# Dividing attention probabilities in the transposing product instead of on GpSimd

## Chip, cores, metric

One core of a Trainium2 chip. The time is that of one execution on the device in microseconds. Engines are named as the profile names them: PE is TensorE's matmul, PEld its weight load, DVE is VectorE, ACT ScalarE, POOL GpSimd, SP SyncE.

## What is computed

A trunk of two layers over 1024 tokens of width 1024. Layer 0 mixes tokens with softmax attention (8 query heads of 128, 2 key/value heads), layer 1 with a gated delta rule; a gated MLP follows each. The change lies in the attention of layer 0:

```
q = apply_axial_rope(rmsnorm(q, q_norm), rope) * (ATT_HEAD_DIM ** -0.5)
k = apply_axial_rope(rmsnorm(k, k_norm), rope)
...
s = jnp.einsum('bqkgd,bskd->bkgqs', q_blk, k)
p = jax.nn.softmax(s, axis=-1)
return jnp.einsum('bkgqs,bskd->bqkgd', p, v)
...
o = o * jax.nn.sigmoid(gate.astype(jnp.float32))
```

## The kernel before

The program runs its stages one after the other on one core; a scheduling layer sets each engine's order of instructions from the order in which they are recorded, the dependences and priorities. Large products are made of pairs: a float32 value is split into a high part of type float32r and a low part (`split`, lines 108 to 110: a cast on ScalarE, a subtraction on VectorE), and three products high x high, high x low, low x high are added in PSUM. Products of plain float32 tiles are also used, for instance at line 513 in the delta-rule layer, where weights and moving operand are 128x128 tiles.

The attention's core is the class `Heads`. A group is one head and one half of its 1024 queries, so there are 16; a group has four tiles of 128 queries. For each tile `scores` (from line 1231) makes the 128x1024 scores by six products of 512 columns (line 1243), VectorE takes their maximum (1246) and a tiny product of it (1247), ScalarE the exponential with its row sums (1249), VectorE the reciprocal of the sums (1251), and GpSimd multiplies the 128x1024 tile p by it (1252). `run` (from 1271) goes over the groups and, in each, over 8 blocks of 128 keys. In blocks 0, 1, 3 and 4 it makes one tile of scores of the next group; in each block it transposes the four 128x128 pieces of p into one PSUM bank (1285), and the bank is split into the pair ph, pl (1288, recorded at lines 109 and 110). `weigh` (1254 to 1269) multiplies a pair with the values by three products of 512 columns (1263), two blocks after the pair was made (`LAG = 2`). After the eighth block VectorE multiplies by the gate (1268), and the result is split.

The first group's scores are made before `run`, between the gate projections of heads 1 to 4 (line 320); the gates are emptied from PSUM by ScalarE at line 291. Tiles of the names base4 to base7 (the profile prints "base") hold the first group's p.

```
for i in range(4):
    nc.tensor.transpose(out=pt[:, i * P:(i + 1) * P], in_=self.ps[g][i][:, j * P:(j + 1) * P],
                        identity=t.ident)
```

Of the kernel before, what the change touches and what calls it, by code (L numbers as in the profile page):

```python
# [9 lines left out]
F32 = mybir.dt.float32  # L10
F32R = mybir.dt.float32r
F16 = mybir.dt.float16
AF = mybir.ActivationFunctionType
ALU = mybir.AluOpType
# [4 lines left out]
P = 128  # L19
# [22 lines left out]
class Trunk:  # L42
    def __init__(self, ctx, tc, ap):
        self.tc, self.nc, self.ap = tc, tc.nc, ap
        nc = self.nc
        pool = lambda **k: ctx.enter_context(tc.tile_pool(reuse_waits="tile", **k))
        tc.cur_priority += 1000000
        self.const = pool(name="const", bufs=1)
        self.dram = pool(name="dram", bufs=1, space=DRAM)
        self.mm = pool(name="mm", bufs=2, space=PSUM)  # L50
        self.ring = "sp"
        self.wp = pool(name="wp", bufs=3)
        self.bp = pool(name="base", bufs=1)
        self.ones = self.const.tile([P, 1], F32, name="ones")
        nc.vector.memset(self.ones, 1.0)
        self.ident = self.load("ident", [P, P])
        self.power = self.const.tile([P, 16], F32, name="power")
        nc.vector.memset(self.power, -0.5)
        self.gain_mix = self.load("norm_mix", [P, 2, KT])
        self.gain_ffn = self.load("norm_ffn", [P, 2, KT])  # L60
        self.gain_final = self.load("norm_final", [P, KT])
# [785 lines left out]
    def run(self, out, start, stop):  # L847
        nc, tc = self.nc, self.tc
        self.psum = self.banks(sp=4)
        if start > 0:  # L850
            if start % 2:
                self.open_operands()
            self.open_h()
            for k in range(KT):
                nc.sync.dma_start(out=self.h[k], in_=self.ap["xT"][k])
                for i, hs in enumerate(HALVES):
                    self.squares(self.h[k][:, hs], hs, k)
        stages = [self.attention, lambda: self.ffn_layer(0), self.gdn, lambda: self.ffn_layer(1)]
        for f in stages[start:stop]:
            f()  # L860
        if stop == 5:
            self.norm(self.h, self.gain_final,
                      out=lambda k, i, y: nc.sync.dma_start(out=out[k][:, HALVES[i]], in_=y))
        else:
            for k in range(KT):
                nc.sync.dma_start(out=out[k], in_=self.h[k])
        self.hp.close()
        if stop % 2 and stop < 5:
            self.ops.close()
        self.psum.close()  # L870
# [335 lines left out]
class Heads:  # L1206


    def __init__(self, trunk, qd, gd, ks, vh, vl, scale, tmp):
        self.t, self.nc = trunk, trunk.nc  # L1210
        self.qd, self.gd, self.ks, self.vh, self.vl, self.scale, self.tmp = qd, gd, ks, vh, vl, scale, tmp
        self.groups = [(h, i) for h in range(NH) for i in range(2)]
        self.qs, self.sgs, self.ps, self.accs, self.waiting, self.ys = {}, {}, {0: []}, {}, [], []

    def queries(self, g, pair):
        h, half = self.groups[g]
        q = self.tmp.tile([P, S], F32, name="t")[:, :H2]
        self.nc.sync.dma_start(out=q, in_=self.qd[h][:, HALVES[half]])
        self.qs[g] = pair
        self.t.split(q, *pair)  # L1220
# [10 lines left out]
    def scores(self, g, p):  # L1231

        nc = self.nc
        h, half = self.groups[g]
        i = len(self.ps[g])
        self.ps[g].append(p)
        kh, kl = self.ks[h // 4]
        qh, ql = self.qs[g]
        acc = self.t.big()
        tok = slice(i * P, (i + 1) * P)  # L1240
        for n, (a, b) in enumerate(((qh, kh), (qh, kl), (ql, kh))):
            for s in HALVES:
                nc.tensor.matmul(acc[:, s], lhsT=a[:, tok], rhs=b[:, s], start=n == 0, stop=n == 2)
        i += 4 * half
        m = self.tmp.tile([P, 4], F32, name="m", bufs=14)
        nc.vector.tensor_reduce(out=m[:, 0:1], in_=acc, op=ALU.max, axis=AX.X)
        nc.vector.scalar_tensor_tensor(out=m[:, 1:2], in0=m[:, 0:1], scalar=-1.0, in1=self.scale[:, h, i:i + 1],
                                       op0=ALU.mult, op1=ALU.mult)
        nc.scalar.activation(out=p, in_=acc, func=AF.Exp, scale=self.scale[:, h, i:i + 1], bias=m[:, 1:2],
                             accum_out=m[:, 2:3])  # L1250
        nc.vector.reciprocal(out=m[:, 3:4], in_=m[:, 2:3])
        nc.gpsimd.tensor_scalar(out=p, in0=p, scalar1=m[:, 3:4], scalar2=1.0, op0=ALU.mult, op1=ALU.mult)

    def weigh(self):

# [15 lines left out]
    def run(self, olo, qp, ptp):  # L1271
        nc, t = self.nc, self.t
        self.ys = [(t.base(h), olo.tile([P, S], F32R, name=f"ol{h}")) for h in range(NH)]
        self.gate(0)
        for g, (h, half) in enumerate(self.groups):
            if g + 1 < len(self.groups):
                self.queries(g + 1, t.pair(qp, "q", H2))
                self.gate(g + 1)
            self.ps[g + 1] = []
            for j in range(NC):  # L1280
                if g + 1 < len(self.groups) and j in (0, 1, 3, 4):
                    self.scores(g + 1, qp.tile([P, S], F32, name="p", bufs=8))
                pt = t.bank()
                for i in range(4):
                    nc.tensor.transpose(out=pt[:, i * P:(i + 1) * P], in_=self.ps[g][i][:, j * P:(j + 1) * P],
                                        identity=t.ident)
                self.waiting.append((g, j, t.pair(ptp, "p", H2)))
                t.split(pt, *self.waiting[-1][2])
                if len(self.waiting) > LAG:
                    self.weigh()  # L1290
            del self.ps[g]
        while self.waiting:
            self.weigh()
        return self.ys
# [97 lines left out]
```

## Time and profile before

| | us |
|---|---|
| median of 3 runs | 3449.74 (3447.62 to 3450.36) |
| the profiled execution | 3439.26 |
| its span in the profile | 3437.5 |
| attention's groups (in the profile) | 291 to 529 |

The span is what the instructions of the program take from the first start to the last end. In the rows, out<-in are the tiles written and read, xN the number of instructions merged or grouped, and <- in brackets what ended an engine's idle time. PE rows overlap, since products are pipelined; the distance from one start to the next is what one takes from the stream.

### The profile page before, as it was taken

What the parts mean: (1) busy time and instruction counts of PE and PEld (TensorE: products, weight loads), DVE (VectorE), ACT (ScalarE), POOL (GpSimd) and SP (SyncE); (2) the same over time, 40 slices, a digit from 0 to 9 for tenths busy, and PEclk for the clock granted to TensorE, in tenths of its full rate; (3) what the DMA queues carried; (4) which work ended last, traced back from release to release, by engine and by line L of the source; (5) the groups of instructions that cost most, each with busy time, mean ns of one, the idle gap of its engine ahead of it and who ended that gap; (6) DMA issues with size and microseconds to landing.
All of it is one profiled execution on the core that took longest, in us unless ns stands there. A gap on an engine that the chain in (4) does not pass through costs nothing. (4 is left out here: it accounts for less than half of the span.)

```text
span 3437.5 us, 54135 instructions
## 1 busy us (share of the span) xinstructions
PE 3247.3 (94%) x19690; PEld 2620.0 (76%) x19690; DVE 2495.2 (73%) x4235; ACT 1741.5 (51%) x3224; POOL 842.4 (25%) x919
## 2 busy tenths in 40 slices
PE   7999999899999998899999999999898989999998
PEld 6877788677777876677777777777676867777786
DVE  5335886887776875778778787877853787777695
ACT  4235664544454454565555556666532544544453
POOL 1111330444442002121221212222120144444100
PEclk9999999999999999999999999999999999999999
DMA  3331006333324642332342424334356623332743
GB/s 127 104 113 59 32 31 191 122 106 111 112 94 168 218 129 65 102 111 88 113 126 81 136 92 130 102 113 132 102 175 206 204 98 110 101 105 92 244 132 109
DMA packets 249802, 411.20 MB, mean 120 GB/s; under 512 B 25536, under 2 KB 76096, under 8 KB 249536
## 3 DMA queue, kind: packets, MB, share of 16 engines
q1 hardware_dynamic: 249536, 407.76, 36.6%
q8 instruction: 155, 2.54, 0.3%
q14 instruction: 111, 0.91, 0.1%
HBM read 294.80 MB, written 107.61 MB: 117 GB/s over the span
## 5 line engine op out<-in xcount | busy, mean ns | idle before, releaser
L134 PE MATMUL mm<-base,wh 128*128 128x512 f32 x1248 | 480.1, 412 | 10.0 <-ACT base L109 5.9
L109 ACT CAST wh<-w_raw 128x512 fp32r<-128x512 f32 x275 | 169.9, 619 | 296.7 <-PE mm L134 175.6
L110 DVE TENSOR_TENSOR wl<-w_raw,wh 128x512 fp32r<-128x512 f32 x275 | 193.2, 707 | 138.2 <-ACT wh L109 137.1
L134 PE MATMUL mm<-yh,wh 128*128 128x512 f32 x736 | 282.6, 413 | 5.3 <-ACT t L291 2.7
L134 PE MATMUL mm<-yh,wl 128*128 128x512 f32 x736 | 280.6, 410 | 1.0 <-DVE wl L110 1.0
L134 PE MATMUL mm<-yl,wh 128*128 128x512 f32 x736 | 279.3, 408 | 0.3 <-POOL yl L110 0.2
L134 PEld LDWEIGHTS mm<-base,wh 128*128 128x128 f32 x1248 | 238.3, 191 | 49.6 <-ACT base L109 6.3
L153 POOL TENSOR_TENSOR rs<-rs,power 128x8 f32<-128x8 f32 (+2 forms) x38 | 63.8, 1679 | 824.8 <-DVE rs L152 824.7
L134 PE MATMUL mm<-base,wl 128*128 128x512 f32 x624 | 257.3, 412 | 6.4 <-DVE wl L110 6.4
L703 POOL TENSOR_SCALAR kd<-c,yds 128x128 f32<-128x128 f32 x224 | 95.2, 437 | 635.0 <-PE cp L732 444.8
L109 ACT CAST wh<-a 128x512 fp32r<-128x512 f32 x164 | 101.8, 622 | 256.7 <-PE mm L134 122.6
L109 ACT CAST wh<-s 128x512 fp32r<-128x512 f32 x212 | 131.4, 620 | 183.6 <-PE sp L134 87.3
L134 PE MATMUL sp<-base,wh 128*128 128x512 f32 (+1 forms) x672 | 211.5, 372 | 12.6 <-ACT wh L109 12.6
L448 DVE SCALAR_TENSOR_TENSOR t<-mm,gdn_cw,t 128x1023 f32<-128x1023 f32 (+1 forms) x128 | 163.1, 1276 | 6.8 <-ACT t L445 6.1
L134 PEld LDWEIGHTS mm<-yh,wh 128*128 128x128 f32 x736 | 140.6, 193 | 29.3 <-ACT t L291 3.6
L134 PEld LDWEIGHTS mm<-yl,wh 128*128 128x128 f32 x736 | 140.8, 192 | 27.8 <-POOL yl L110 1.6
L134 PEld LDWEIGHTS mm<-yh,wl 128*128 128x128 f32 x736 | 140.8, 191 | 26.5 <-DVE wl L110 1.7
L134 PE MATMUL sp<-base,wl 128*128 128x512 f32 (+1 forms) x432 | 157.7, 365 | 1.4 <-DVE wl L110 0.9
L134 PEld LDWEIGHTS sp<-base,wh 128*128 128x128 f32 x672 | 127.7, 190 | 34.3 <-ACT wh L109 13.0
L110 DVE TENSOR_TENSOR wl<-s,wh 128x512 fp32r<-128x512 f32 x170 | 142.0, 836 | 12.3 <-ACT wh L109 12.2
L978 POOL TENSOR_TENSOR s<-a,a 128x512 f32<-128x512 f32 x80 | 108.5, 1356 | 159.0 <-DVE s L978 106.0
L134 PEld LDWEIGHTS mm<-base,wl 128*128 128x128 f32 x624 | 119.1, 191 | 27.2 <-DVE wl L110 7.2
(522 smaller groups left out, 9362.4 us busy)
## 6 DMA issues: line engine op xcount, KB each, us to landing
a<-in_ffn_up_dram SPq DMA_DIRECT2D x160, 256.0 KB, 2.8
c<-pk SPq DMA_DIRECT2D x128, 320.0 KB, 3.1
w_raw<-in_gdn_in_dram SPq DMA_DIRECT2D x100, 256.0 KB, 2.8
g_t<-t SPq DMA_DIRECT2D x88, 256.0 KB, 2.0
raw<-g_t SPq DMA_DIRECT2D x88, 256.0 KB, 2.6
w_raw<-in_gdn_out_dram SPq DMA_DIRECT2D x68, 256.0 KB, 3.6
g<-t SPq DMA_DIRECT2D x66, 256.0 KB, 2.1
raw<-g SPq DMA_DIRECT2D x66, 256.0 KB, 2.8
```

The source lines that it names most:

```text
L109: self.nc.scalar.copy(out=hi, in_=src)
L110: (engine or self.nc.vector).tensor_tensor(out=lo, in0=src, in1=hi.bitcast(F32), op=ALU.subtract)
L134: self.nc.tensor.matmul(acc if one else acc[:, hs], lhsT=a, rhs=y[:, hs], start=(first and not onto and k + t == 0), stop=(last and k == n ...
L153: nc.gpsimd.tensor_tensor(out=r, in0=v, in1=self.power[:, :w], op=ALU.pow)
L448: nc.vector.scalar_tensor_tensor(out=o, in0=a, scalar=c[:, i:i + 1], in1=o, op0=ALU.mult, op1=ALU.add)
L703: nc.gpsimd.tensor_scalar(out=kd[:, e], in0=kn, scalar1=col(self.yds, e), scalar2=1.0, op0=ALU.mult, op1=ALU.mult)
L978: e.tensor_tensor(out=s[i], in0=x, in1=z, op=op)
```

## The change

The division by the row sums leaves GpSimd. For each tile ScalarE scales the rows of the 128x128 identity by the reciprocals, which gives a diagonal matrix `inv` (eight buffers, two groups). The four pieces of p are no longer transposed against the identity but multiplied with that diagonal by an ordinary float32 product: p transposed times the diagonal is the transposed tile with each query's column divided by its sum.

```diff
--- before.py
+++ after.py
@@ -1211,6 +1211,7 @@
         self.qd, self.gd, self.ks, self.vh, self.vl, self.scale, self.tmp = qd, gd, ks, vh, vl, scale, tmp
         self.groups = [(h, i) for h in range(NH) for i in range(2)]
         self.qs, self.sgs, self.ps, self.accs, self.waiting, self.ys = {}, {}, {0: []}, {}, [], []
+        self.invs = {}
 
     def queries(self, g, pair):
         h, half = self.groups[g]
@@ -1249,7 +1250,9 @@
         nc.scalar.activation(out=p, in_=acc, func=AF.Exp, scale=self.scale[:, h, i:i + 1], bias=m[:, 1:2],
                              accum_out=m[:, 2:3])
         nc.vector.reciprocal(out=m[:, 3:4], in_=m[:, 2:3])
-        nc.gpsimd.tensor_scalar(out=p, in0=p, scalar1=m[:, 3:4], scalar2=1.0, op0=ALU.mult, op1=ALU.mult)
+        inv = self.tmp.tile([P, P], F32, name="inv", bufs=8)
+        nc.scalar.activation(out=inv, in_=self.t.ident, func=AF.Identity, scale=m[:, 3:4])
+        self.invs.setdefault(g, []).append(inv)
 
     def weigh(self):
 
@@ -1282,13 +1285,14 @@
                     self.scores(g + 1, qp.tile([P, S], F32, name="p", bufs=8))
                 pt = t.bank()
                 for i in range(4):
-                    nc.tensor.transpose(out=pt[:, i * P:(i + 1) * P], in_=self.ps[g][i][:, j * P:(j + 1) * P],
-                                        identity=t.ident)
+
+                    nc.tensor.matmul(pt[:, i * P:(i + 1) * P], lhsT=self.ps[g][i][:, j * P:(j + 1) * P],
+                                     rhs=self.invs[g][i], start=True, stop=True)
                 self.waiting.append((g, j, t.pair(ptp, "p", H2)))
                 t.split(pt, *self.waiting[-1][2])
                 if len(self.waiting) > LAG:
                     self.weigh()
-            del self.ps[g]
+            del self.ps[g], self.invs[g]
         while self.waiting:
             self.weigh()
         return self.ys
```

Two places where the order of instructions differs follow; the numbers in the names are buffers. The first is ScalarE in the middle of the attention stage, over half a group: first before, then of the change (p is an exponential, ph the high part of a transposed bank, qh that of the next queries, base2 or base3 that of a finished head).

```order
L1249 ACTIVATE p_3048,m_3056<-mm_3049,m_3056,scale_102 128x1024
L109 CAST ph_3093<-sp_3088 128x512
L109 CAST ph_3109<-sp_3104 128x512
L1249 ACTIVATE p_3074,m_3082<-mm_3075,m_3082,scale_102 128x1024
L109 CAST base2_2046<-t_3100 128x512
L109 CAST qh_3205<-t_3207 128x512
L109 CAST ph_3136<-sp_3131 128x512
L1249 ACTIVATE p_3117,m_3125<-mm_3118,m_3125,scale_102 128x1024
L109 CAST ph_3162<-sp_3157 128x512
L109 CAST ph_3174<-sp_3169 128x512
L1249 ACTIVATE p_3143,m_3151<-mm_3144,m_3151,scale_102 128x1024
```

```order
L1250 ACTIVATE p_3414,m_3422<-mm_3415,m_3422,scale_102 128x1024
L1254 ACTIVATE inv_3427<-ident_71,m_3422 128x128
L109 CAST ph_3461<-sp_3456 128x512
L1250 ACTIVATE p_3441,m_3449<-mm_3442,m_3449,scale_102 128x1024
L109 CAST ph_3477<-sp_3472 128x512
L1254 ACTIVATE inv_3454<-ident_71,m_3449 128x128
L109 CAST base3_2052<-t_3468 128x512
L109 CAST qh_3575<-t_3577 128x512
L109 CAST ph_3505<-sp_3500 128x512
L1250 ACTIVATE p_3485,m_3493<-mm_3486,m_3493,scale_102 128x1024
L109 CAST ph_3532<-sp_3527 128x512
L1254 ACTIVATE inv_3498<-ident_71,m_3493 128x128
```

An `inv` follows each exponential: one right behind its own, the others behind one cast of a bank.

The second place is VectorE in the same stage, around the low half of the queries (ql), first before, then of the change (the reduction is of the scores' maxima, pl the low part of a transposed bank).

```order
L1246 TENSOR_REDUCE m_2656<-mm_2649 128x1
L1251 RECIPROCAL m_2630<-m_2630 128x1
L110 TENSOR_TENSOR pl_2668<-sp_2662,ph_2667 128x512
L1247 SCALAR_TENSOR_TENSOR m_2656<-m_2656,scale_102 128x1
L110 TENSOR_TENSOR ql_2711<-t_2712,qh_2710 128x512
L110 TENSOR_TENSOR pl_2680<-sp_2674,ph_2679 128x512
L1251 RECIPROCAL m_2656<-m_2656 128x1
```

```order
L1247 TENSOR_REDUCE m_2648<-mm_2641 128x1
L110 TENSOR_TENSOR ql_2731<-t_2732,qh_2730 128x512
L1248 SCALAR_TENSOR_TENSOR m_2648<-m_2648,scale_102 128x1
L110 TENSOR_TENSOR pl_2661<-sp_2655,ph_2660 128x512
L1247 TENSOR_REDUCE m_2675<-mm_2668 128x1
L1252 RECIPROCAL m_2648<-m_2648 128x1
L1248 SCALAR_TENSOR_TENSOR m_2675<-m_2675,scale_102 128x1
L110 TENSOR_TENSOR pl_2688<-sp_2682,ph_2687 128x512
L1252 RECIPROCAL m_2675<-m_2675 128x1
```

ql stood behind the second tiny product and ahead of one bank's low part; now it stands ahead of the first tiny product, one bank earlier.

## Rows read from the trace of the kernel before

**Rows 1.** By stretches: start:end, length, busy us per engine (instructions), clock, DMA.

```profile
291.00:529.00 238.00, 232.85 (x1245) 188.93 (x1246) 204.50 (x353) 160.21 (x280) 68.24 (x60) 1.00 0.10 35
529.00:560.00 31.00, 30.07 (x133) 24.55 (x132) 15.97 (x24) 11.06 (x18) 0.00 (x0) 1.00 0.70 223
```

**Rows 2.** Waits in 291 to 529 us: us, times, longest.

```profile
ACT p L1249 <- DVE m L1247: 44.4, 56, 1.4
...
PEld sp L1263 <- DVE pl L110: 8.8, 17, 0.7
```

**Rows 3.** Groups in 291 to 529 us: count, busy us, mean ns, idle before.

```profile
L1252 POOL TENSOR_SCALAR p<-p,m 128x1024 f32<-128x1024 f32 x60 | 68.2, 1138 | 189.6 <-DVE m L1251 127.0 <-PE sp L1285 57.0 <-DVE m L1247 5.6
...
L1251 DVE RECIPROCAL m<-m 128x1 f32<-128x1 f32 x60 | 9.5, 158 | 9.7 <-ACT p L1249 9.7
```

**Rows 4.** Timeline of PE, four transposes: start us, length us, instructions merged.

```profile
513.69 0.60 PE L1285 MATMUL sp<-ident,p 128*128 128x128 f32 x4
514.04 0.48 PE L1263 MATMUL sp<-ph,vh 128*128 128x512 f32 x1
514.36 0.40 PE L1263 MATMUL sp<-pl,vh 128*128 128x512 f32 x1
514.60 0.39 PE L1263 MATMUL sp<-ph,vl 128*128 128x512 f32 x1
```

**Rows 5.** Timeline of PE at line 513, ordinary products of this shape.

```profile
1393.11 1.05 PE L513 MATMUL sp<-t 128*128 128x128 f32 x8
1393.92 0.48 PE L134 MATMUL mm<-base,wl 128*128 128x512 f32 x1
1394.23 0.39 PE L134 MATMUL mm<-yh,wl 128*128 128x512 f32 x1
...
1394.95 1.16 PE L513 MATMUL sp<-t 128*128 128x128 f32 x8
1395.86 0.48 PE L134 MATMUL mm<-base,wh 128*128 128x512 f32 x1
```

**Rows 6.** By source line: 513 (ordinary products), 1285 (transposes); min/median/max ns.

```profile
L513 PE MATMUL sp<-t x256: 270/275/426, 1386.6 to 2401.3; 128*128 128x128 f32 x128
...
L1285 PE MATMUL sp<-ident,p x480: 270/272/330, 304.3 to 526.7; 128*128 128x128 f32 x160
```

**Rows 7.** Timeline of PE: late products, first and last of twelve; last group.

```profile
334.55 0.50 PE L1263 MATMUL sp<-pl,vh 128*128 128x512 f32 x1 [0.20 <-DVE pl L110]
...
501.11 0.47 PE L1263 MATMUL sp<-ph,vh 128*128 128x512 f32 x1
501.86 0.50 PE L1263 MATMUL sp<-pl,vh 128*128 128x512 f32 x1 [0.28 <-DVE pl L110]
...
517.10 0.49 PE L1285 MATMUL sp<-ident,p 128*128 128x128 f32 x3
518.72 0.33 PE L1285 MATMUL sp<-ident,p 128*128 128x128 f32 x1 [1.13 <-POOL p L1252]
```

**Rows 8.** Timelines of VectorE and GpSimd, line 1247 with and without GpSimd.

```profile
347.90 0.59 DVE L1247 SCALAR_TENSOR_TENSOR m<-m,scale 128x1 f32<-128x1 f32 x1
...
347.36 1.13 POOL L1252 TENSOR_SCALAR p<-p,m 128x1024 f32<-128x1024 f32 x1 [2.58 <-DVE m L1251]
...
353.72 0.15 DVE L1247 SCALAR_TENSOR_TENSOR m<-m,scale 128x1 f32<-128x1 f32 x1
```

**Rows 9.** Timeline of PE behind the early transposes, two of four places.

```profile
227.46 0.49 PE L1285 MATMUL sp<-ident,base 128*128 128x128 f32 x3
228.85 0.73 PE L134 MATMUL mm<-yh,wh 128*128 128x512 f32 x2 [0.90 <-ACT t L291]
...
291.07 0.49 PE L1263 MATMUL sp<-ph,vh 128*128 128x512 f32 x1 [1.26 <-ACT ph L109]
```

**Rows 10.** Groups of ScalarE of the shape 128x128: count, busy us, mean ns.

```profile
L718 ACT ACTIVATE o<-cp,egc 128x128 f32<-128x128 f32 x112 | 35.5, 365 | 27.4 <-DVE r L714 16.4 <-PE mm L134 9.0 <-PE ip L674 1.2
...
L484 ACT ACTIVATE sq<-h 128x128 f32<-128x128 f32 x64 | 20.1, 313 | 1.2
```

## Prediction

> **What bounds the kernel now.** I read the page's summary first, then a table by stretches, then the waits and groups of the attention stretch, and last the timeline of TensorE there. The summary gives averages over stages with different limits, so it only says that PE is the busiest engine and GpSimd the idlest; the table by stretches says more [rows 1]. From 291 to 529 us, where nearly all the changed instructions run, PE is busy 232.9 of 238 us at a granted clock of 1.00 (the 2.4 GHz level), VectorE 204.5, ScalarE 160.2, GpSimd 68.2, and DMA is at 0.10. In the waits of that stretch ScalarE waits 44.4 us for VectorE, but PE's own waits add up to little: the largest is 8.8 us, of its weight loads, for the low half of a transposed bank [rows 2]. So PE's own stream of instructions sets the end of this stretch, and the next stretch follows it with PE busy 30.1 of 31 us. The 60 divisions that go from this stretch take 68.2 us [rows 3], but on an engine for which PE hardly waits.
>
> **The change, part by part.**
>
> *Transposes become products.* The loops make 16 groups of 8 key blocks of 4 query tiles: 512 transposes, in 128 banks of four. In the profile a transpose is one row: 480 that read the tiles p, which are 15 of the groups x 32 [rows 6]. An ordinary float32 product of the same shape, 128x128 weights and 128 columns, is two rows: line 513 makes 8 x 2 x 2 x 4 = 128 products in the code, and the profile has 256 rows [rows 6]. Durations in these rows overlap, so I price by starts. Four transposes in the stage: from 513.69 to the next product at 514.04, 0.35 us, and from that product to the one after it 0.32 [rows 4]: 0.67 together. Of this 0.24 is the product's own pace (514.36 to 514.60), so a transpose takes 0.43 / 4 = 0.108. Four ordinary products at line 513: from 1393.11 to 1393.92, 0.81, and 0.31 behind them, 1.12 together [rows 5]; without the 0.24 that is 0.22 for one. The next bank of line 513 takes 0.91 from 1394.95 to 1395.86, and 1.22 with 0.31 behind it [rows 5]. So a bank costs +0.45 or +0.55 us more; eight rows at the transposes' pace of 0.108 would make it +0.43. I take +0.47, near the lower sample: the new products stand right behind other products in the stage, as those at 1393.11 do, where the first of the eight rows is not late.
>
> Not all 128 banks pay. Four early banks get their first three transposes while the gates are projected, and PE is idle right after: 0.90 us until ScalarE has emptied the gate (three times), 1.26 until a bank is cast (once) [rows 9]. Three products instead of three transposes are 3 x (0.22 - 0.108) = 0.34 us longer and fit into that. So 500 products pay, 125 banks: 125 x 0.47 = **+58.8 us** (bounds +54 and +69).
>
> The Trainium skill's page "TensorE: Matmul & The Clock Gate", section Terms, says that the transpose mode is 4 times faster for float32, which speaks against this change even more than the rows do. By that a product would cost 0.43 us for a transpose's 0.108, and the term would be some +162 us instead of +58.8 (an estimate from that page and the row). The trace differs: 0.22 against 0.108, a ratio of 2.0; so the sum goes by the rows, and the rule is a rival below.
>
> *The division on GpSimd goes:* 64 instructions of 1.14 us [rows 3], 60 of them in the stage. The direct wait of PE for it comes once, in the last group: from 517.10 to 518.72 it is 1.62 us where three transposes need 0.32 [rows 7], so **-1.3 us**. Indirect: once a group VectorE's tiny 128x1 product of line 1247 takes 0.59 us while GpSimd divides (347.36 to 348.49), where it takes 0.15 without [rows 8]; behind it in VectorE's queue stand the low half of the queries and then the low half of a bank, and PE waits for that one. The PE timeline shows it: the product on the low half is late 12 times, first at 334.55 and last at 501.86, where it starts 0.75 us behind the one before it instead of 0.32 [rows 7]. The first is late by a little less; 12 x 0.42 = **-5.0 us**. Both go: the division is gone, and PE is slower, so that the others have more time. Bounds: 0 (the waits come back at another place) and -7.1 (two waits of 0.4 at the start of the stage also go).
>
> *A diagonal is made on ScalarE:* 64 activations of 128x128, bounded by two rows of the same shape, 0.31 us from SBUF and 0.37 from PSUM with a scale per partition [rows 10]; I take 0.31, since the identity lies in SBUF. 60 x 0.31 = 19 us brings ScalarE from 160 to 179 us in a stage that will be 291 us long: beside other work, so nothing of it is on the path. If that cover were gone it would be all 19. The order of instructions shows no further table load. The activation waits for the reciprocal, and behind it in ScalarE's queue stand casts of transposed banks, for which PE waits. In the order three of the four in a group stand behind a cast, one right behind its own exponential; there ScalarE sits through the reciprocal (0.16 us) [rows 3]. PE uses a bank two key blocks after it was transposed (LAG = 2), and with the products a key block takes 1.6 us or more, so half a us of delay in the queue is covered. I put **+1.0 us** for the stage; bounds 0 and +28 (60 x (0.31 + 0.16), if all of it, activation and reciprocal, reached PE).
>
> *Moved:* VectorE's and ScalarE's order inside a group, as the two excerpts show: the queries' low half stands one bank earlier. PE's order differs only at the start of the stage, SyncE's not at all, and no DMA is added or moved. The 8 new tiles of 512 bytes a partition change no order behind the stage. All of it at 0, inside the bounds above. Behind the stage everything begins later by the same time.
>
> **Sum.** +58.8 - 6.3 + 1.0 = +53.5 us. The profiled execution took 3439.26 us (span 3437.5) and would become 3492.8. The median of the runs, 3449.74, is 10.5 us above it; the change is added to the median: **3503 us**. The stage from 291 to 529 us becomes about 291 us long.
>
> **The rivals.**
>
> *A: ScalarE's queue becomes late.* Each diagonal blocks ScalarE until VectorE has made the reciprocal, banks are cast late, PE waits. For it: ScalarE already waits 44.4 us for VectorE's line 1247 in this stage [rows 2], and it will wait for line 1251's successor as well. Against it: 179 of 291 us, and LAG = 2. It decides once the delay passes the two key blocks of lead. Price: +28 in place of +1.0, so +80.5: about 3530 us.
>
> *B: the products cost four times a transpose,* two rows of twice a transpose's time each. From the rows: 500 x 3 x 0.108 = +162, less 6.3: about 3605 us. For it would speak a bank whose rows each wait for their weights, which no sample here shows; against it stand both samples [rows 5]. The rule behind it is that of the Trainium skill's "TensorE: Matmul & The Clock Gate" (Terms).
>
> *C, on the other side: the products run as the transposes did,* one row each at 0.108 us, because the weights and shapes are the same and only the moving operand is another. Then nothing is added and the waits of 6.3 to 7.1 us go: 3443 to 3444 us, at the edge of faster. It decides from a price of some +0.05 us a bank downward (6.3 / 125). Against it: line 513 has two rows for one product [rows 6]. That the change does not do what it says is excluded by the order of instructions, where all 512 products read the diagonal and no division is left. That PE's extra time hides behind VectorE is no rival of its own: PE has about 5 us of 238 idle [rows 1], so it cannot hide 58.
>
> **How the numbers follow.** Forecast 0.87, A 0.07, B 0.02, C 0.04. Under the forecast the term of the products runs from 54 to 69 and the waits from -7.1 to +1 and a few more, so +47 to +70; the low end and the middle are likelier, and run to run the kernel before spread over 2.7 us. The range 3496 to 3520 (+46 to +70) keeps some 0.93 of the forecast, 0.81 in all, and leaves A, B and C out. A difference under 0.2%, 6.9 us, is about what a measurement of this kernel cannot tell from no change. Slower 0.96 (forecast, A, B); C lies on that edge, so 0.02 same and 0.02 faster.
>
> **What would show it.** Right: 1024 matmul rows where 512 were, banks of eight rows in 0.81 us at 1.00 clock, the stage near 291 us, no 0.7 us start-to-start at the first product behind a bank, line 1248 (the tiny product, 1247 before) at 0.15 us throughout, ScalarE under 65% busy in the stage. Wrong: one row per product, or a price far from 0.2 us each; PE idle before the weighing products for ScalarE's casts in most key blocks (A); a stage whose length is not that of PE's rows.

## The result and the profile after

| | us |
|---|---|
| before, median of 4 runs | 3450.05 (3447.62 to 3450.39) |
| the change, median of 4 runs | 3496.43 (3485.55 to 3501.94) |
| ratio | 1.0132, 95% interval 1.0103 to 1.0162 |
| the change again, measured later | 3494.04 against 3445.28; ratio 1.0144 (1.0129 to 1.0159) |

The kernel became slower by 1.3 to 1.4%, as forecast in kind. By the ratio that is +45.5 us, just under the low end of the range (+46); the medians differ by 46.4, just above it. The forecast was +53.5.

"Stage" means from here on the time from the first weighing product (line 1263, 1266 in the change) to the first product behind the last one. To see where it goes, I took each TensorE row's distance to the next start and sorted these by kind: turning p (the transposes, or the products that replace them), weighing with the values, and scores. A wait is what a distance has above the median of its kind with the same neighbours, if that is over 60 ns.

| stage, us | length | turning p | weighing | scores | waits |
|---|---|---|---|---|---|
| before | 237.9 | 44.2 | 100.1 | 84.2 | 9.4 |
| the change | 285.5 | 101.0 | 99.5 | 84.4 | 0.5 |

So the stage grew by 47.6 us: 56.4 for the rows, less 8.8 of waits. That is the difference of the medians (46.4, and 48.8 when measured again) to within the scatter of the runs. The rest of the program lasts between 3193 and 3215 us in the profiles of all kernels of this study (span less stage), at mean granted clocks of 0.987 to 0.979: single executions differ by that, and the change's own profile is a long one.

The table by stretches of the change, which answers to [rows 1] (the columns are the same):

```profile
291.00:577.00 286.00, 285.50 (x1746) 251.83 (x1746) 201.62 (x354) 182.23 (x340) 0.00 (x0) 1.00 0.09 30
577.00:608.00 31.00, 30.08 (x133) 24.61 (x132) 15.80 (x24) 11.15 (x19) 0.00 (x0) 1.00 0.70 220
```

PE is idle for half a us in 286, still at a clock of 1.00; the stretch behind it is as it was. The rows of the new products by source line, the answer to [rows 6], and four of them in the timeline of PE, the answer to [rows 4]:

```profile
L1289 PE MATMUL sp<-inv,p x960: 270/275/295, 307.5 to 574.5; 128*128 128x128 f32 x192
```

```profile
402.13 1.05 PE L1289 MATMUL sp<-inv,p 128*128 128x128 f32 x8
402.94 0.48 PE L1266 MATMUL sp<-ph,vh 128*128 128x512 f32 x1
403.26 0.40 PE L1266 MATMUL sp<-pl,vh 128*128 128x512 f32 x1
```

960 rows where 480 were, and 0.81 + 0.32 us where 0.35 + 0.32 stood. The groups and waits of the stretch 291 to 577 us, the answers to [rows 2, 3, 10] (groups: count, busy us, mean ns, idle before; waits: us, times, longest):

```profile
L1254 ACT ACTIVATE inv<-ident,m 128x128 f32<-128x128 f32 x60 | 24.4, 407 | 4.5 <-DVE m L1252 4.5
...
L1248 DVE SCALAR_TENSOR_TENSOR m<-m,scale 128x1 f32<-128x1 f32 x60 | 9.4, 156 | 1.0
```

```profile
PEld sp L1266 <- ACT ph L109: 1.1, 1, 1.1
PE sp L1266 <- ACT ph L109: 0.9, 1, 0.9
...
PEld sp L1266 <- DVE pl L110: 0.7, 2, 0.5
PE sp L1266 <- DVE pl L110: 0.2, 1, 0.2
PEld sp L1289 <- ACT inv L1254: 0.2, 1, 0.2
```

A diagonal takes 0.41 us, more than either row had suggested, and PE waits 0.2 us in all for one. The tiny product of VectorE takes 0.156 us throughout, and PE's waits for the low halves, 8.8 us of weight loads before, are down to 0.7. For a cast of a bank PE waits once, ahead of the stage's first product.

### The profile page after: what moved, and what is told of

Read it like the earlier page. It is cut to its first block, busy times and chain, and to the rows that moved or that the text cites. A ratio compares the mean times of both kernels' runs of the same rounds, so it can differ in the third digit from the quotient of the medians.

```text
span 3500.2 us, 54956 instructions
## 1 busy us (share of the span) xinstructions
PE 3307.2 (94%) x20202; PEld 2686.2 (77%) x20202; DVE 2495.7 (71%) x4235; ACT 1765.5 (50%) x3288; POOL 764.4 (22%) x855
```

## Experiments

The questions: is the cost that of the products alone (theory 1), and what made PE's 9.4 us of waits before go, GpSimd's silence (W1) or PE's slower pace (W2)? The rivals are A (ScalarE's queue) and costs outside the stage.

### The change again

No edit. 

> The changed kernel once more, for its spread. Stage means, here and in all runs, the time from the first weighing product (line 1263 before, 1266 in the change) to the first product behind the last one: 237.9 us before, 285.5 in the change. Theory 1, what moves the time lies in the stage and the rest is the same program: stage 285.5 +- 0.5 again, and the median 44 to 50 us over the kernel before, with single runs up to 10 us apart because the stretches where TensorE's granted clock is 0.5 lie elsewhere in each execution. Rival, the change also costs outside its stage (in the profiles the rest grew by 14.7 us): median over +55 us.

Measured: stage 285.5 us with 0.5 of waits, ratio 1.0144 (1.0129 to 1.0159), median 48.8 us over the kernel before, single runs 3491.39 to 3498.87. Theory 1 holds: the stage gives 47.6 of the 48.8 us, and nothing outside it stands clear of the scatter of the runs.

### Ordinary products, the division still on GpSimd

```diff
 # in the kernel before
-nc.tensor.transpose(out=pt[...], in_=self.ps[g][i][...], identity=t.ident)
+nc.tensor.matmul(pt[...], lhsT=self.ps[g][i][...], rhs=t.ident, start=True, stop=True)
```

> The kernel before with ordinary products against the plain identity in place of the transposes; the division stays on GpSimd and no diagonal is made. Both theories: the 500 products of the stage cost 0.1136 us more each, +56.8. Theory W1, PE's waits before (9.4 us in the stage) came from GpSimd's division holding up VectorE: the waits stay, stage 237.9 + 56.8 = about 294 to 295 us. Theory W2, they came from PE being too fast for the others and vanish once it is slower: stage about 285.5 to 287, as in the change.

Measured: stage 285.8 us, turning 101.0, waits 0.6; ratio 1.0151 (1.0136 to 1.0166). This edit alone makes the whole slowdown. The waits are gone although GpSimd still divides (60 divisions in the stage), as W2 has it. But this does not show that a slower PE covers a VectorE that is held up. The edit also changed the order: VectorE works here in the change's order, with the queries' low half one bank earlier, but for a dozen instructions of the whole program. The groups of VectorE in the middle of the stage (304 to 510 us) show that no tiny product is held by a division any more. A division holds the low half of a finished head (ol) instead, which takes 0.91 us where it takes 0.69 in the change, and PE does not wait for it:

```profile
L110 DVE TENSOR_TENSOR ol<-t,base 128x512 fp32r<-128x512 f32 x11 | 10.0, 905 | 0.0
...
L1247 DVE SCALAR_TENSOR_TENSOR m<-m,scale 128x1 f32<-128x1 f32 x46 | 7.1, 155 | 0.7
```

### No division at all

```diff
 # in the kernel before
-nc.gpsimd.tensor_scalar(out=p, in0=p, scalar1=m[:, 3:4], scalar2=1.0, op0=ALU.mult, op1=ALU.mult)
```

> The kernel before without the division on GpSimd and with nothing in its place; this leaves the division of the probabilities out of the computation. Transposes as before, no diagonal. Theory W1, the waits came from the division: they go, stage about 229 to 230 us, 8 to 9 us faster. Theory W2, they came from PE's pace: the stage keeps all but the 1.3 us of the last group, about 236 to 237 us.

Measured: stage 230.0 us, waits 1.3; ratio 0.9980 (0.9970 to 0.9989). Here PE keeps its pace and GpSimd is silent, and the waits are gone as well: W1. The order on VectorE and ScalarE is the kernel before's but for about a dozen instructions of the whole program, so here it is the division that made the waits. VectorE's tiny product, 304 to 510 us:

```profile
L1247 DVE SCALAR_TENSOR_TENSOR m<-m,scale 128x1 f32<-128x1 f32 x57 | 8.6, 150 | 0.0
```

So neither theory excludes the other. The waits come with both together, the division on GpSimd and the transposes' pace, and removing either removes them. The change removed both and could gain the 8 us only once. With this order, that is also about the most that taking the division off GpSimd is worth.

### Diagonals made, not used

```diff
 # in the change
-nc.tensor.matmul(pt[...], lhsT=self.ps[g][i][...], rhs=self.invs[g][i], start=True, stop=True)
+nc.tensor.transpose(out=pt[...], in_=self.ps[g][i][...], identity=t.ident)
```

> The change with the transposes against the identity put back: the diagonals are made on ScalarE and nobody reads them, so the division of the probabilities is left out. Against the run without any division it shows what the 64 activations and their waits for the reciprocal cost. Theory 1, they are covered: within 1 us of that run's stage. Rival A of the prediction, ScalarE's queue becomes late, here against a PE that is not slowed: 5 to 28 us longer than that run's stage.

Measured: stage 230.0 us, waits 1.3, the same as without diagonals; ratio 0.9966 (0.9954 to 0.9979). ScalarE's additional work is covered even with a fast PE, in the order that this program got. The diagonals' waits for the reciprocal, 300 to 520 us, which leave the stage as long as it was:

```profile
ACT inv L1254 <- DVE m L1252: 4.6, 27, 0.4
```

### Products in every second key block

```diff
 # in the change
+if j % 2:
     nc.tensor.matmul(pt[...], lhsT=self.ps[g][i][...], rhs=self.invs[g][i], start=True, stop=True)
+else:
+    nc.tensor.transpose(out=pt[...], in_=self.ps[g][i][...], identity=t.ident)
```

> The change with products by the diagonal in every second key block (j odd) and plain transposes in the others; this leaves half of the probabilities undivided. Theory 1, the price is that of the products and proportional to their number: 64 banks in the stage x 0.454 us = +29.1 on the 230.0 us of the run without division and without products, and the waits of 1.3 us there shrink: stage 258 to 259.2 us. Rival, the price comes with mixing the two kinds of turning or with the diagonal being ready late: stage over 262 us, or PE idle before line 1289.

Measured, one run: stage 257.6 us, turning 72.8, waits 0.9; 3471.94 us. By source line, products (1289) and transposes (1292):

```profile
L1289 PE MATMUL sp<-inv,p x480: 270/275/275, 308.8 to 545.8; 128*128 128x128 f32 x160
```

```profile
L1292 PE MATMUL sp<-ident,p x240: 270/272/296, 306.2 to 544.2; 128*128 128x128 f32 x120
```

With the first group's rows, it has 252 more rows of turning than the run without a division (752 against 500) and is 27.6 us longer, 0.110 us for each; the change has 500 more and is 55.4 us longer, 0.111 each. The price is proportional to the number of products. The stage lies 0.4 us under theory 1's band, which counted 64 banks where the rows show 63 (252 / 4).

### Products in float32r

```diff
 # in the change
-nc.scalar.activation(out=p, in_=acc, func=AF.Exp, ...)
+nc.scalar.activation(out=p.bitcast(F32R), in_=acc, func=AF.Exp, ...)
-nc.scalar.activation(out=inv, in_=self.t.ident, ...)
+nc.scalar.activation(out=inv.bitcast(F32R), in_=self.t.ident, ...)
-nc.tensor.matmul(pt[...], lhsT=self.ps[g][i][...], rhs=self.invs[g][i], ...)
+nc.tensor.matmul(pt[...], lhsT=self.ps[g][i][...].bitcast(F32R), rhs=self.invs[g][i].bitcast(F32R), ...)
```

> The change with the probabilities and the diagonal written and multiplied as float32r, which rounds them, to see what the type does to the price. Theory 1, an ordinary product is two rows because its operands are float32: here one row each, 512 rows, at most 0.108 us, stage 205 to 230 us. Rival, a product outside transpose mode costs 0.22 us whatever its type: 1024 rows, stage about 285 us.

Measured, one run: 3466.22 us, stage 254.3. By source line, and a bank in the timeline of PE:

```profile
L1289 PE MATMUL sp<-inv,p x480: 218/275/330, 311.1 to 546.2; 128*128 128x128 f32 x160
```

```profile
401.55 0.56 PE L1289 MATMUL sp<-inv,p 128*128 128x128 f32 x4
401.94 0.44 PE L1266 MATMUL sp<-ph,vh 128*128 128x512 f32 x1
402.22 0.40 PE L1266 MATMUL sp<-pl,vh 128*128 128x512 f32 x1
```

One row each, and 0.39 + 0.28 us for a bank with the product behind it, 0.67 as for the transposes: two rows are the float32 type's, not the ordinary product's. But the stage is 24 us longer than without the division, outside what either theory gave. Its rows sum to 229.4 us; its waits are 24.9. The waits of 300 to 540 us:

```profile
PEld sp L1266 <- DVE pl L110: 16.3, 30, 0.8
...
ACT inv L1254 <- DVE m L1252: 5.6, 17, 1.4
PEld sp L1266 <- ACT ph L109: 5.3, 15, 0.4
```

And one of the places in the timeline of all engines:

```profile
403.82 0.56 PE L1289 MATMUL sp<-inv,p 128*128 128x128 f32 x4
404.02 0.15 DVE L1252 RECIPROCAL m<-m 128x1 f32<-128x1 f32 x1
404.13 0.16 DVE L1248 SCALAR_TENSOR_TENSOR m<-m,scale 128x1 f32<-128x1 f32 x1
404.20 0.40 ACT L1254 ACTIVATE inv<-ident,m 128x128 fp32r<-128x128 f32 x1
404.21 0.69 DVE L110 TENSOR_TENSOR pl<-sp,ph 128x512 fp32r<-128x512 f32 x1
...
404.23 0.50 PE L1266 MATMUL sp<-ph,vh 128*128 128x512 f32 x1
...
404.95 0.51 PE L1266 MATMUL sp<-pl,vh 128*128 128x512 f32 x1 [0.23 <-DVE pl L110]
```

VectorE and ScalarE work here in the change's own order, row for row. A low half (404.21) stands behind a reduction, a reciprocal and a tiny product, and PE, 0.46 us faster in every bank, waits for it. In the change, with the same order and the slower products, the waits are 0.5 us. (In this execution 3.4 us at the start of the stage have a granted clock of 0.50 (the 1.2 GHz level), which the change's stage has not; that is far less than the 24 us.)

### PE reads the diagonals at the transposes' price

```diff
 # in the change
-nc.vector.reciprocal(out=m[:, 3:4], in_=m[:, 2:3])
+nc.vector.tensor_scalar(out=m[:, 3:4], in0=m[:, 2:3], scalar1=0.0, scalar2=1.0, op0=ALU.mult, op1=ALU.add)
-nc.tensor.matmul(pt[...], lhsT=self.ps[g][i][...], rhs=self.invs[g][i], start=True, stop=True)
+nc.tensor.transpose(out=pt[...], in_=self.ps[g][i][...], identity=self.invs[g][i])
```

> The change with the 64 diagonals made as before but with ones in them (the reciprocal is replaced by 0 x sum + 1, on the same engine), and PE transposing against them in transpose mode; this leaves the division of the probabilities out. So PE depends on the diagonals as in the change, at the transposes' price; ScalarE's and VectorE's order is nearly that of the run with unused diagonals. Theory O, the 24.9 us of waits in the float32r run come from the order in which its (and the change's) VectorE and ScalarE work, which a slower PE covers: here the waits stay near 1.3 us, stage 230 to 232 us. Theory D, they come from PE's dependence on the diagonals: stage over 245 us.

Measured, one run: stage 230.4 us, waits 1.2; 3432.43 us. By source line:

```profile
L1288 PE MATMUL sp<-inv,p x480: 270/272/273, 305.1 to 520.0; 128*128 128x128 f32 x160
```

Theory D falls: PE's dependence on the diagonals costs nothing. The order is what is left of the differences to the float32r run, together with the float32r type: the durations of the exponential and the diagonal are the same (1.20 and 0.40 us), and PE's weight loads take 190 ns there and 141 here, but PE's rows sum to about the same, 229.4 and 229.2 us. A run with the change's order and plain transposes was not made, since the order follows from the instructions; that the order is the cause is argued from the timeline above, not shown.

### The tiny product on ScalarE

```diff
 # in the kernel before
-nc.vector.scalar_tensor_tensor(out=m[:, 1:2], in0=m[:, 0:1], scalar=-1.0, in1=self.scale[:, h, i:i + 1], ...)
+nc.scalar.activation(out=m[:, 1:2], in_=m[:, 0:1], func=AF.Identity, scale=self.t.nscale[:, h, i:i + 1])
```

> The kernel before with one thing moved: the 128x1 product of maximum and scale goes from VectorE to ScalarE (one activation ahead of the exponential, with a negated copy of the scales), so that GpSimd's division has no tiny VectorE product to hold up. Theory 1, that held-up product is what makes PE late once a group: the 12 waits of 0.52 us go, stage 237.9 - 6 = about 232 us, the 1.3 us of the last group stay, and the median is 4 to 8 us under the kernel before. Rival, GpSimd's division holds up other VectorE instructions as well (the low halves, the reductions) or ScalarE's longer queue takes it back: stage 235 to 240 us, no difference in the median.

Measured: stage 240.9 us, waits 6.8, scores 88.5 where 84.2 were; ratio 1.0001 (0.9989 to 1.0014). The rival holds, with a stage 0.9 us over its band. The order changed with the edit, and GpSimd's division now meets another VectorE instruction, the low half of a finished head, which read 770 ns before. VectorE's groups, 300 to 520 us:

```profile
L110 DVE TENSOR_TENSOR ol<-t,base 128x512 fp32r<-128x512 f32 x14 | 20.1, 1435 | 4.5 <-ACT base L109 4.5
```

PE waits for VectorE and for ScalarE (300 to 530 us), so which of the rival's two reasons weighs more is not separated:

```profile
PEld sp L1264 <- DVE pl L110: 8.1, 14, 0.6
...
PEld sp L1264 <- ACT ph L109: 4.8, 13, 0.4
```

### The third tile's division on ScalarE

```diff
 # in the kernel before
+if i % 4 == 2:
+    nc.scalar.activation(out=p, in_=p, func=AF.Identity, scale=m[:, 3:4])
+else:
     nc.gpsimd.tensor_scalar(out=p, in0=p, scalar1=m[:, 3:4], ...)
```

> The kernel before with the division of one tile in four (the third of a group, whose division overlaps the late tiny product) on ScalarE instead of GpSimd. Theory 1, that one division makes PE late: the 12 late products go, stage about 232 us, ScalarE 19 us busier and covered. Rival, ScalarE's 1.2 us in the middle of the casts makes others late: stage 236 us or more.

Measured, one run: stage 240.0 us, waits 9.5; 3445.07 us. The rival holds. The 12 late products of the kernel before are gone, as theory 1 has it: the tiny product ahead of the queries' low half takes 0.15 us. But casts now wait behind ScalarE's 1.15 us, and PE is late by 0.52 us once a group at another place, behind the scores:

```profile
426.02 1.15 ACT L1253 ACTIVATE p<-p,m 128x1024 f32<-128x1024 f32 x1
...
428.26 1.55 ACT L109 CAST ph<-sp 128x512 fp32r<-128x512 f32 x3
...
428.89 0.50 PE L1266 MATMUL sp<-ph,vh 128*128 128x512 f32 x1 [0.38 <-ACT ph L109]
```

### The division on the gate

```diff
 # in the kernel before, in run(); no division of p
+if j == 5:
+    bc = t.bank()
+    for i, m in enumerate(self.ms.pop(g)):
+        nc.tensor.transpose(out=bc[:, i * P:(i + 1) * P], in_=m[:, 3:4].to_broadcast([P, P]), identity=t.ident)
+    nc.vector.tensor_tensor(out=self.sgs[g], in0=self.sgs[g], in1=bc, op=ALU.mult)
```

> The kernel before with the division taken off the probabilities and put on the gate: in the sixth key block of a group four transposes spread the reciprocals over the partitions in one PSUM bank, and VectorE multiplies the gate tile (128x512) by it. Theory 1, from the run without division: stage 230.0 + 16 groups x 0.44 us of PE = 237 us, and VectorE's 16 x 0.7 us stay covered: 1 us under the kernel before in the stage, no measurable difference in the median. Rival, the additional PSUM bank and VectorE's work make PE wait: stage over 240 us.

Measured: stage 238.6 us, of it 7.0 for the new transposes and 1.9 of waits; ratio 0.9999 (0.9988 to 1.0009). That lies between theory 1's 237 us and the rival's 240: what the waits give back, the transposes take, and the median does not differ.

### The division in quarters

```diff
 # in the kernel before
-nc.gpsimd.tensor_scalar(out=p, in0=p, scalar1=m[:, 3:4], scalar2=1.0, op0=ALU.mult, op1=ALU.mult)
+for c in range(4):
+    cs = slice(c * S // 4, (c + 1) * S // 4)
+    nc.gpsimd.tensor_scalar(out=p[:, cs], in0=p[:, cs], scalar1=m[:, 3:4], scalar2=1.0, op0=ALU.mult, op1=ALU.mult)
```

> The kernel before with each division on GpSimd made as four instructions of 256 columns instead of one of 1024; the order on the other engines is nearly unchanged. Theory 1, VectorE's tiny product is held up for as long as one GpSimd instruction lasts: at most 0.3 us now instead of 1.1, most of the 12 late products go, stage 232 to 235 us, median 3 to 6 us under the kernel before. Rival, the tiny product waits for the whole division all the same, since the next quarter starts at once: stage 237 to 239 us, no difference.

Measured: stage 230.7 us, waits 1.6; ratio **0.9967** (0.9956 to 0.9978), median 3435.44 against 3445.46. This beats both kernels: in the stage nearly all that leaving the division out gave, with the division done. The rival falls. Theory 1 holds, and the gain is larger than it gave (232 to 235 us in the stage, 3 to 6 in the median). Of the 10.0 us between the medians the stage explains 7.2; where the rest comes from the runs do not show. The order on VectorE and ScalarE is the kernel before's but for two instructions each in the whole program, so this run changes the division's pieces and little else. The place of [rows 8] in this run, VectorE and GpSimd:

```profile
347.93 0.40 DVE L1247 SCALAR_TENSOR_TENSOR m<-m,scale 128x1 f32<-128x1 f32 x1
348.25 0.68 DVE L110 TENSOR_TENSOR ql<-t,qh 128x512 fp32r<-128x512 f32 x1
348.85 0.68 DVE L110 TENSOR_TENSOR pl<-sp,ph 128x512 fp32r<-128x512 f32 x1
```

```profile
347.39 2.35 POOL L1254 TENSOR_SCALAR p<-p,m 128x256 f32<-128x256 f32 x4 [1.69 <-PE sp L1287]
```

GpSimd now works 2.35 us on this tile (1.86 in the median), and yet the tiny product takes 0.40 us instead of 0.59. It need only wait for the quarter that runs: the records of the 27 held products of the kernel before end 1 to 7 ns behind the end of a whole division, those of the 11 held ones here 3 to 5 ns behind the end of a quarter.

The prediction saw one held product in a group; there are two. The other is held longer, and ends with its division as well (kernel before):

```profile
355.97 1.13 POOL L1252 TENSOR_SCALAR p<-p,m 128x1024 f32<-128x1024 f32 x1 [4.60 <-PE sp L1285]
...
356.31 0.80 DVE L1247 SCALAR_TENSOR_TENSOR m<-m,scale 128x1 f32<-128x1 f32 x1
```

Here that one takes 0.15 us, and 0.41 us is the longest (min/median/max ns in this run):

```profile
L1247 DVE SCALAR_TENSOR_TENSOR m<-m,scale x64: 138/150/408, 217.4 to 509.6; 128x1 f32<-128x1 f32 x64
```

How much of the 7.2 us each of the two gave is not separated. Not all of VectorE's work is held: the low halves of banks, which it reads from PSUM, take 0.68 us in the kernel before whether a division runs beside them (60) or not (67). The tiny product's mean over the stage falls from 401 to 198 ns (VectorE's groups, 304 to 520 us, before and here):

```profile
L1247 DVE SCALAR_TENSOR_TENSOR m<-m,scale 128x1 f32<-128x1 f32 x57 | 22.9, 401 | 0.0
```

```profile
L1247 DVE SCALAR_TENSOR_TENSOR m<-m,scale 128x1 f32<-128x1 f32 x58 | 11.5, 198 | 0.0
```

The wait for GpSimd in the last group goes too (1.3 us before, 0.1 here).

## Why the prediction was right and wrong

Right: the sign and the path. PE bounds the stage; an ordinary float32 product is two rows; the division that goes was worth only PE's waits; ScalarE's diagonals are covered. What the prediction named as signs stands in the profile: twice the rows, banks of 0.81 us, the tiny product at 0.156 us, ScalarE busy 182.2 of 286 us (64%).

Wrong is the size, 53.5 against 47.6 us in the stage, and with it the range. The step that failed is the sizing of the sum's terms; three were off, all to the same side:

- "125 x 0.47 = +58.8 us": the rows of the stage grew by 56.4 us, 0.45 a bank. That is the lower of the two samples of line 513; the 0.02 put on top of it, a step towards the higher sample (+0.55), was not paid.
- "12 x 0.42 = -5.0" and "-1.3": the waits that went were 8.8 us, more than the bound of -7.1, and with them the gain was put 2.5 us too low. I had counted the late start of a product, not the 0.10 us by which the product behind it is late as well, because its weight load begins late: 0.10 us behind the late product's start (349.85 against 349.75) where elsewhere the two begin together. So it is 0.33 us to the next start behind the late ones and 0.23 elsewhere: 12 x 0.52 = 6.2. The rest is the start of the stage, which I had kept for the bound only, and that was too small by the same oversight.
- "+1.0 us" for ScalarE's queue: 0 (the same stage with and without the diagonals, 230.0 us). That a diagonal takes 0.41 us and not 0.31 cost nothing.

The low end of the range, +46, needed the lowest price together with the highest gain. The price came low in its bounds (56.4 in 54 to 69) and the gain beyond its bound, so that the stage's +47.6 lies just inside the range and the measured +45.5 (ratio) to +48.8 around its end. On which side of it a measurement falls is the runs' scatter.

The account of the waits was also incomplete: two tiny products in a group were held, not one, and the longer of them, 0.80 us, is not in it. That both go with the division made this harmless for the sum.

Of the rivals, B falls: 0.22 us for a product, not 0.43. The rule on the transpose mode in the Trainium skill's "TensorE: Matmul & The Clock Gate" (Terms) differs from these runs, where the transpose is 2.0 times faster in float32. A did not happen, and the run with unused diagonals shows that ScalarE's queue is covered even at the transposes' pace, in that run's order. What the float32r run puts in doubt is another entry, "Moved", the order inside a group, put at 0: with the change's order and a PE at the transposes' pace the stage has 24.9 us of waits, mostly for VectorE's low halves (weight loads wait 16.3 us for these, 5.3 for casts). The change, in the same order, has 0.5 us of waits at its slower pace. The prediction had named that cover ("PE is slower, so that the others have more time") for the old waits and for ScalarE's queue, but gave VectorE's new order 0 without working it out; that it came out at 0 was in part luck. By the same run C was priced wrongly: the one run with products at the transposes' pace had a stage of 254.3 us, 16 more than before, and 3466 us, not 3443.

## What to carry to other kernels

Before work is folded into a matrix product, count the rows that the product takes in the operand's type: here a float32 transpose of one row became a product of two, and on the engine that bounds the stage 500 of them cost 56 us, where the 68 us taken off GpSimd were worth 8. Work on an engine off the path is worth, if removed, what others wait for it; a run without that work shows how much. Where a long GpSimd instruction holds up short VectorE ones, cutting it into pieces can be cheaper than moving it, and any move changes the order, which can bring the wait back elsewhere.

## What was not expected of the hardware

- A tiny 128x1 product of VectorE is held by a GpSimd instruction over 128x1024 for up to 0.65 us (0.80 at most in place of 0.15 in the timeline of the kernel before) and ends within 7 ns of it; cutting GpSimd's instruction in four (0.48 us each in the median, 1.86 for the four of a tile against 1.13 for the whole) shortens this.
- A float32r product of 128 columns has the pace of a float32 transpose (0.67 us for four and the product behind them, in both).
- Scaling a 128x128 tile per partition on ScalarE from SBUF takes 0.41 us, where squares of the same shape take 0.31.
